# Weight sums of the first feed-forward in 2 KB tiles, norm squares on ScalarE, bounded leads for weights, and 54 instead of 53 small tiles

## The chip, the core and the metric

One core of a Trainium2 chip runs the whole program. The metric is the device time of one execution in microseconds (us). The engines are named as in the profile: PE is TensorE (PEld its weight loads), DVE is VectorE, ACT is ScalarE, POOL is GpSimd, SP is the queue from which the loads are issued.

## The reference

A decoder layer over 512 tokens of width 1024, in float32:

```
x = x + 0.5 * swiglu(rmsnorm(x, ffn1_norm), ffn1_wgu, ffn1_wdown)   # d_ff 2816
h = rmsnorm(x, mix_norm);  z = h @ w_in         # q, k, v, conv (2 x 1024), gates (2 x 1024)
a = sliding_window_attention(q, k, v, sinks) @ attn_proj
c = silu(layernorm(causal_conv31(glu(zc)))) @ conv_proj
x = x + (sigmoid(ga) * a + sigmoid(gb) * c) @ w_out
x = x + 0.5 * swiglu(rmsnorm(x, ffn2_norm), ffn2_wgu, ffn2_wdown)
x = x + sigmoid(rmsnorm(x, ple_gate_norm) @ ple_gate_w) * rmsnorm(p @ ple_proj, ple_norm)
```

where `swiglu(h, w_gu, w_down)` is `(silu(g) * u) @ w_down` with `g, u` the halves of `h @ w_gu`, and `rmsnorm` divides by the root of the mean square over the 1024 features.

## The kernel before

Features lie on the 128 partitions: x is eight tiles of 128 x 512 (features x tokens). Every float32 operand of a product is split into an upper and a lower half in a rounded format (ACT copies src to hi, DVE or POOL computes lo = src - hi), and `mm3` issues three matmuls for a product: hi x hi, lo x hi, hi x lo. A weight piece is a load of 128 x 1024 into a raw tile and two 4 KB tiles, whi and wlo, of class hi and lo.

**Pairs.** In a feed-forward the first blocks of 128 columns of g and u are done plainly (four in the first, two in the second), the others in pairs of blocks (`pair`, line 952) by a scheme with seven products in place of eight. A pair loads four raw pieces A[f, kh] (three in class raw, which has three slots, the fourth in class k, which has two), builds four sums of them (`add`, line 965; each in two halves of 128 x 512, tiles f_s, on DVE or POOL as the planner likes), and splits seven "forms" (`form`, line 971): 1 and 2 and 4 are raw pieces, 6, 5, 7 and 3 are the sums. They are multiplied two at a time in the order (1, 2), (6, 5), (7, 3), 4: `both` runs g and u, and each `times` is 12 matmuls of 256 columns. A form holds one hi and one lo slot, of three each, from its split to its last matmul. The moving operands are the h tiles and activations that `sums` (line 881) prepares once. After 8, 16 and 22 blocks `down` (line 1035) multiplies by w_down, in eight groups, one for each x tile.

**Norms.** `next_norm` (line 1070) gives the last `down` of a feed-forward, and the output product of the mixer, a function `after(o)`. It splits the new x[o] into h tiles and has `SumSq.add` (line 802) square x[o] on POOL and add it on POOL to a tile in SBUF. The sum over partitions follows as small matmuls (mean_rstd; names _n_cs in the trace) and is spread over the partitions, or as matmuls with a matrix of 1/1024 (wide_rstd, for the last norm). The very first norm does it otherwise: squares on ACT (n_sq), added by DVE into a PSUM bank (n_acc).

**The planner.** No order is written out. `record()` lists all operations; `deadlines` (line 366) works back a latest start for each from the PE order of the pass before; `simulate` (line 395) lets each engine take the ready operation with the earliest due time, and `plan` (line 640) makes five passes and keeps the one with the shortest simulated span. Then every operation is issued in that order (line 1495: all rows carry the line of this loop, L1498, so they are told apart by their tiles). `can` (line 435) decides whether an operation may take its output tiles: a slot of the class must be free (`SLOTS`, line 648: 53 of class a, 2 KB each; 8 PSUM banks); of class a, one, three or six must stay free beside it when its slack is over 2, 6 or 20 us; and hi and lo tiles aren't taken when the slack is over AHEAD = 22 us. Class a holds the h tiles and prepared activations (hi and lo, 16 tiles each in a feed-forward), rb, the f_s sums and the tiles of a pair's evictions (g, u, U: two each). DVE and POOL instructions on SBUF are planned as excluding each other.

Of the kernel before, what the change touches and what calls it, by code (L numbers as in the profile page):

```python
# [12 lines left out]
AF = mybir.ActivationFunctionType  # L13
ALU = mybir.AluOpType
# [29 lines left out]
"""  # L44
POOLCH = (0, 2, 4)
WARM = 9
AHEAD = 22
MARGIN = 0.0

CAPS = {"cz": 2, "ct": 4}  # L50
# [175 lines left out]
class Program:  # L226
# [69 lines left out]
    def costs(self, op, eng=None):  # L296

        ins = op.reads
        o = op.writes[0] if op.writes else None
        n = max([v.free() for v in ([o] if o else []) + ins])  # L300
        psum = any(v.vt.cls == "ps" for v in op.writes + ins)
        eng = eng or op.eng
        op.lock = eng == "POOL"
        op.fset = None
        op.dma = 0.0
        vecs = sum(isinstance(v, V) for v in [*op.a[3:], *(v for n, v in op.k.items() if n != "accum_out")])
        if eng == "PE":
            if op.what == "transpose":
                op.cost, op.lat = 0.112, 0.3
            else:  # L310
                n = op.a[2].free()
                if op.a[2].vt.dtype == F32R:
                    op.cost, op.lat = (0.2275, 0.3) if n > 256 else (0.121, 0.3)
                else:
                    op.cost, op.lat = max(0.15, n * 0.00167), 0.35
        elif eng == "DVE":
            op.lat = 0.15
            if op.what == "tensor_tensor":
                op.cost = 0.065 + n * 1.055e-3
            elif op.what == "scalar_tensor_tensor":  # L320
                op.cost = 0.08 + n * 1.12e-3
            elif op.what == "tensor_tensor_reduce":
                op.cost = 0.28 + n * 1.02e-3
            elif op.what in ("reduce_sum", "tensor_reduce"):
                op.cost = 0.08 + n * 1.03e-3
            else:
                op.cost = 0.08 + n * (1.25e-3 if psum else 0.9e-3)
            op.lock = not psum and op.what not in ("tensor_tensor_reduce", "reduce_sum", "tensor_reduce", "reciprocal")
        elif op.what == "dma_start" and eng == "ACT":
            op.cost, op.lat = 0.5, 2.6  # L330
        elif eng == "ACT":
            op.cost, op.lat = 0.07 + n * 0.88e-3, 0.17
            op.cost += 0.094 * vecs
            if "accum_out" in op.k:
                op.cost += 0.1
            f = op.a[2].name if len(op.a) > 2 else "Copy"
            op.fset = SETS.get(f)
        elif eng == "POOL":
            op.lat = 0.15
            if op.what == "tensor_tensor":  # L340
                op.cost = 0.14 + n * 2.1e-3
            elif op.what == "tensor_scalar":
                op.cost = 0.25 + n * 0.8e-3
            else:
                op.cost = 0.12 + n * 1.0e-3
        else:
            op.cost, op.lat = 0.47, 0.0
            v = (op.writes + op.reads)[0]
            op.dma = v.free() * v.shape[0] * 4 / 240e3
# [45 lines left out]
def simulate(prog, slots):  # L395
# [39 lines left out]
    def can(op, slack):  # L435
        for vt in op.outs:
            if vt.slot is None:
                break
        else:
            return True  # L440
        need = {}
        for v in op.writes:
            vt = v.vt
            if vt.slot is None:
                need.setdefault(vt.cls, {})[vt] = True
        for c, vts in need.items():
            spare = 0
            if c == "a":
                if slack > 400.0:
                    return False  # L450
                spare = 0 if slack < 2.0 else 1 if slack < 6 else 3 if slack < 20 else 6
            if c in ("hi", "lo") and slack > AHEAD:
                return False
            if len(free[c]) < len(vts) + spare:
                return False
            if any(vt.kind and inuse[vt.kind] >= CAPS[vt.kind] for vt in vts):
                return False
        return True
# [89 lines left out]
    while left:  # L548
# [23 lines left out]
        for e in ENGINES:  # L572
            if busy[e] > t + 1e-9:
                continue
            if e == "PE":
                pe(t)
                continue
            best = None
            if e == "SP":
                state = len(ready[e]), len(free["raw"]), len(free["a"])  # L580
                if state == idle_sp:
                    continue
                idle_sp = state
            for key, _, op in ready[e]:
                if best is not None and key >= best[0]:
                    break
                if op.outs and op.outs[0].after > t:
                    continue
                if e == "ACT" and op.fset and op.fset != aset:
                    key += 1.5  # L590
                elif e == "DVE":
                    if op.flex:
                        key += 5.0
                    if op.lock:
                        key += max(0.0, lock_pool - t)
                if best is not None and key >= best[0]:
                    continue
                if can(op, op.ls + lag - t):
                    best = (key, op)
            if best is None:  # L600
                continue
            op = best[1]
            slack = op.ls + lag - t
            if hold[e] > t and slack > 10.0 and op.cost > 0.3:
                continue
            if e == "POOL" and slack > 8.0:
                if hold[e] > t:
                    push(hold[e], "wake")
                    continue
                if lock_dve > t and any(o.lock and ls + lag - t < 4.0 for ls, _, o in ready["DVE"]):  # L610
                    push(lock_dve, "wake")
                    continue
            idle_sp = None if e == "SP" else idle_sp
            ready[e].remove((op.ls, op.i, op))
            if op.flex:
                ready["POOL" if e == "DVE" else "DVE"].remove((op.ls, op.i, op))
                op.eng = e
                prog.costs(op)
            launch(op, t)
# [25 lines left out]
    return prog, spans[-1]  # L645


SLOTS = {"a": 53, "o": 4, "raw": 3, "hi": 3, "lo": 3, "ps": 8, "k": 2, "x": 8, "c": 100000}


def record():
    nc = Program()

    def ps_tile(name):
        return nc.tile(name, [P, S], F32, "ps")

    def ftile(name):
        return nc.tile(name, [P, S], F32, "a")
# [48 lines left out]
    def mm3(ps, w, x, start, stop, first=1, skip=False):  # L707

        nc.tensor.matmul(ps, w[first], x[0], start=start, stop=False, skip_group_check=skip)
        nc.tensor.matmul(ps, w[1 - first], x[0], start=False, stop=False, skip_group_check=skip)  # L710
        nc.tensor.matmul(ps, w[0], x[1], start=False, stop=stop, skip_group_check=skip)

    def part(w, s):
        return w[0][:, s], w[1][:, s]
# [83 lines left out]
    class SumSq:  # L798
# [3 lines left out]
        def add(self, v, on_act=False, accs=1):  # L802
# [11 lines left out]
                eng.tensor_tensor(acc, acc, to, op=ALU.add)  # L814
            self.n += 1


    warm = ps_tile("warm")
    with nc.group("warm"):
# [83 lines left out]
                    forms[f].append((hi[:, j * HS : (j + 1) * HS], lo[:, j * HS : (j + 1) * HS]))  # L903
        return forms

    def ffn(tag, wgu, wdown, h, gain, ss, after, cuts, wide, plain):

# [42 lines left out]
        def pair(i, T, new):  # L952
# [16 lines left out]
                    nc.flex.tensor_tensor(sm[n][c], *ab, op=op)  # L969

            def form(n, src):
                hi = nc.tile(f"whi_{wgu}{i}_{n}", [P, PIECE], F32R, "hi")
                lo = nc.tile(f"wlo_{wgu}{i}_{n}", [P, PIECE], F32R, "lo")
                if isinstance(src, list):
                    for c in range(2):
                        s = slice(c * S, (c + 1) * S)
                        split_into(hi[:, s], lo[:, s], src[c])
                else:
                    split_into(hi, lo, src)
                return hi, lo  # L980
# [13 lines left out]
            def times(m, n, w, b, to, start):  # L994
                with nc.group(f"{tag}_p{n}{i}_{m}"):
                    for k in range(4):
                        c = k * 256 + m * P
                        mm3(to[m], part(w, slice(c, c + P)), b[k], start and k == 0, k == 3, skip=n in (3, 4, 6, 7))

            def both(n1, s1, r1, n2, s2, r2, first):  # L1000
                w1, w2 = form(n1, s1), form(n2, s2)
# [68 lines left out]
    def next_norm(tag, gain):  # L1070
        h, ss = [], SumSq(f"{tag}_ss")

        def after(o):
            h.append(split(f"{tag}_h{o}", x[o], gain[:, o : o + 1]))
            ss.add(x[o])

        return h, ss, after

    h2, ss2, after = next_norm("mix", g_mix)
    ffn("f1", "wgu1", "wd1", h, g_ffn1, ss, after, 4, False, 4)  # L1080


    def proj(tag, key, i, h, nk=KD):
# [365 lines left out]


    h4, ss4, after4 = next_norm("pg", g_gate)
    ffn("f2", "wgu2", "wd2", h3, g_ffn2, ss3, after4, 1, False, 2)


    rb4 = None
# [142 lines left out]
```

## Time and profile before

| what | us |
|---|---|
| median of 3 runs (lowest, highest) | 1183.63 (1183.03, 1185.38) |
| the profiled execution | 1182.44 |
| its span, from the first to the last instruction | 1180.7 |
| PE busy | 1166.4 (99%), 6740 matmuls |
| DVE busy | 984.3 (83%) |
| ACT busy | 630.2 (53%) |
| POOL busy | 492.2 (42%) |

Stages by the span's clock: first feed-forward to 362 us (its pairs from 54 us, with down projections at 94 to 137, 222 to 266 and from 330 us), the mixer to about 798 us, the second feed-forward to about 1133 us, then the last gate. In the rows below, a row of a timeline gives the start, the busy time, the engine, the operation and its tiles, the count, and in brackets the idle time of the engine before it with what ended it. Tiles of the pairs are named f_g8a, f_u8b and so on by the first block of the pair; wlo_wgu and whi_wgu are the halves of a form, f_s a sum, raw_wgu a loaded piece. A matmul's row is longer than its distance to the next one.

### The profile page before, as it was taken

What the parts mean: (1) busy time and instruction counts of PE and PEld (TensorE: products, weight loads), DVE (VectorE), ACT (ScalarE), POOL (GpSimd) and SP (SyncE); (2) the same over time, 40 slices, a digit from 0 to 9 for tenths busy, and PEclk for the clock granted to TensorE, in tenths of its full rate; (3) what the DMA queues carried; (4) which work ended last, traced back from release to release, by engine and by line L of the source; (5) the groups of instructions that cost most, each with busy time, mean ns of one, the idle gap of its engine ahead of it and who ended that gap; (6) DMA issues with size and microseconds to landing.
All of it is one profiled execution on the core that took longest, in us unless ns stands there. A gap on an engine that the chain in (4) does not pass through costs nothing.

```text
span 1180.7 us, 17926 instructions
## 1 busy us (share of the span) xinstructions
PE 1166.4 (99%) x6740; PEld 1029.3 (87%) x6740; DVE 984.3 (83%) x1479; ACT 630.2 (53%) x1117; POOL 492.2 (42%) x444
## 2 busy tenths in 40 slices
PE   9999999999999999999999999999999999999998
PEld 7898899989988888888888888889998999899886
DVE  7996799769986898998999786689966997589876
ACT  7553255415544669989865673445542555245432
POOL 2330442023334896897899600444302241122340
PEclk9999999999999999999999999999999999999999
DMA  7424224333133221222222233232243224222331
GB/s 239 131 72 125 89 91 125 90 100 114 41 106 105 90 90 54 89 72 72 72 90 89 89 91 107 90 125 80 86 151 105 81 90 128 87 92 75 103 107 72
DMA packets 37815, 115.30 MB, mean 98 GB/s; under 512 B 4704, under 2 KB 9440, under 8 KB 37728
## 3 DMA queue, kind: packets, MB, share of 16 engines
q1 hardware_dynamic: 37584, 114.12, 30.4%
q8 instruction: 53, 0.87, 0.3%
q14 instruction: 34, 0.28, 0.1%
q10 hardware_dynamic: 144, 0.03, 0.0%
HBM read 112.04 MB, written 2.10 MB: 97 GB/s over the span
## 4 chain that ended last, share of the span: by engine, by line
PE 87%; DVE 7%; ACT 3%; issue 2%; DMA 1%; SPq 0%; DVEq 0%; ACTq 0%
PE f_d L1498 20%; PE ga L1498 4%; PE ap L1498 4%; PE cp L1498 4%; PE wo L1498 4%; PE cb L1498 3%; PE pg L1498 3%; PE ca L1498 3%; PE gb L1498 2%; DVE wlo_wgu L1498 2%; PE f_g L1498 2%; PE f_u L1498 2%; PE q1b L1498 2%; DVE cz L1498 2%; PE sc L1498 2%
## 5 line engine op out<-in xcount | busy, mean ns | idle before, releaser
L1498 POOL TENSOR_TENSOR f_s<-raw_wgu,raw_wgu 128x512 f32<-128x512 f32 x42 | 73.9, 1770 | 337.6 <-DVE f_d L1498 164.0
L1498 DVE TENSOR_TENSOR wlo_wgu<-f_s,whi_wgu 128x512 fp32r<-128x512 f32 x152 | 136.3, 931 | 15.3 <-ACT whi_wgu L1498 15.1
L1498 ACT ACTIVATE whi_wgu<-raw_wgu 128x1024 fp32r<-128x1024 f32 (+1 forms) x93 | 76.2, 834 | 102.9 <-PE f_d L1498 35.0
L1498 ACT ACTIVATE whi_wgu<-f_s 128x512 fp32r<-128x512 f32 x152 | 88.7, 625 | 58.9 <-PE f_d L1498 13.3
L1498 POOL TENSOR_TENSOR y<-y,ct 128x507 f32<-128x507 f32 (+27 forms) x90 | 114.2, 1292 | 5.8 <-ACT ct L1498 4.2
L1498 DVE TENSOR_TENSOR wlo_wgu<-raw_wgu,whi_wgu 128x1024 fp32r<-128x1024 f32 (+1 forms) x93 | 108.4, 1174 | 7.7 <-ACT whi_wgu L1498 7.2
L1498 DVE SCALAR_TENSOR_TENSOR cz<-u,dww,cz 128x510 f32<-128x510 f32 (+25 forms) x145 | 105.0, 734 | 2.5
L1498 ACT ACTIVATE whi_wd<-raw_wd 128x1024 fp32r<-128x1024 f32 (+1 forms) x48 | 47.4, 987 | 104.4 <-PE f_d L1498 90.5
L1498 DVE TENSOR_TENSOR f_d<-f_d,f_n_rb 128x512 f32<-128x512 f32 x48 | 33.5, 698 | 70.8 <-PE f_d L1498 70.6
L1498 POOL TENSOR_TENSOR f_s<-raw_wgu,f_s 128x512 f32<-128x512 f32 x28 | 46.1, 1650 | 58.0 <-DVE f_us L1498 28.4
L1498 DVE TENSOR_TENSOR wlo_wd<-raw_wd,whi_wd 128x1024 fp32r<-128x1024 f32 (+1 forms) x48 | 54.7, 1140 | 7.3 <-ACT whi_wd L1498 7.3
L1498 ACT ACTIVATE ct<-u,dww 128x505 f32<-128x505 f32 (+28 forms) x90 | 58.3, 702 | 2.2 <-DVE u L1498 2.1
L1498 POOL TENSOR_TENSOR f_s<-f_s,raw_wgu 128x512 f32<-128x512 f32 x24 | 38.8, 1618 | 18.3 <-DVE f_s L1498 6.0
L1498 ACT ACTIVATE f_gs<-f_gs 128x512 f32<-128x512 f32 x44 | 27.5, 626 | 29.6 <-DVE f_gs L1498 29.6
L1498 POOL TENSOR_TENSOR f_ss_sq<-x 128x512 f32<-128x512 f32 x8 | 8.7, 1084 | 80.5 <-DVE x L1498 80.5
L1498 DVE TENSOR_TENSOR f_s<-raw_wgu,raw_wgu 128x512 f32<-128x512 f32 x34 | 35.7, 1054 | 0.7 <-DVE f_a10l L1498 0.4
L1498 DVE SCALAR_TENSOR_TENSOR x<-f_d,x 128x512 f32<-128x512 f32 x48 | 32.7, 688 | 1.1
L1498 ACT ACTIVATE s<-s,m,q_r 128x128 f32<-128x128 f32 x64 | 30.9, 487 | 0.1
L1498 ACT ACTIVATE whi_wzc<-raw_wzc 128x1024 fp32r<-128x1024 f32 x16 | 17.0, 1060 | 26.1 <-issue 9.0
L1498 POOL TENSOR_TENSOR mix_ss_sq<-x 128x512 f32<-128x512 f32 x8 | 10.9, 1363 | 39.8 <-DVE x L1498 39.8
L1498 POOL TENSOR_TENSOR pg_ss_sq<-x 128x512 f32<-128x512 f32 x8 | 12.6, 1572 | 35.8 <-DVE x L1498 35.8
L1498 ACT ACT_TABLE_LOAD x20 | 25.7, 1283 | 1.6 <-PEq L1587 1.2
(1289 smaller groups left out, 4552.3 us busy)
## 6 DMA issues: line engine op xcount, KB each, us to landing
raw_wgu<-in_wgu SPq DMA_DIRECT2D x80, 512.0 KB, 3.7
raw_wd<-in_wd SPq DMA_DIRECT2D x32, 512.0 KB, 4.0
raw_wzc<-in_wzc SPq DMA_DIRECT2D x16, 512.0 KB, 3.6
raw_wzg<-in_wzg SPq DMA_DIRECT2D x16, 512.0 KB, 3.6
raw_wd<-in_wd SPq DMA_DIRECT2D x16, 384.0 KB, 3.2
raw_wgu<-in_wgu SPq DMA_DIRECT2D x32, 128.0 KB, 3.1
raw_wq<-in_wq SPq DMA_DIRECT2D x8, 512.0 KB, 3.5
raw_wap<-in_wap SPq DMA_DIRECT2D x8, 512.0 KB, 3.5
```

Source lines behind the costliest of these rows:

```text
L1498: getattr(engines[op.eng], op.what)(*a, **k)
```

## The change

Five edits. In the first feed-forward (`own` is true there, false in the second) the forms that are sums no longer take a whi and a wlo tile of 4 KB: each half gets its own hi and lo tile of class a, 2 KB each, so four for a form; `times` picks the half. `next_norm` calls `in_psum` in place of `add`: squares on ACT, added by DVE, the running sum in a PSUM bank and the last one in an SBUF tile. The bound on slack is given by class: 16 us for hi and lo, 24 us for raw and k, which had none. Class a has 54 slots. The planner's cost of a matmul is 0.2272 and 0.1197 us in place of 0.2275 and 0.121, and its look at SP's queue is renewed with each new microsecond.

```diff
-AHEAD = 22
+LEAD = {"hi": 16, "lo": 16, "raw": 24.0, "k": 24.0}
-                    op.cost, op.lat = (0.2275, 0.3) if n > 256 else (0.121, 0.3)
+                    op.cost, op.lat = (0.2272, 0.3) if n > 256 else (0.1197, 0.3)
-            if c in ("hi", "lo") and slack > AHEAD:
+            if slack > LEAD.get(c, 1e9):
                 return False
-                state = len(ready[e]), len(free["raw"]), len(free["a"])
+                state = len(ready[e]), len(free["raw"]), len(free["a"]), int(t)
-SLOTS = {"a": 53, "o": 4, "raw": 3, "hi": 3, "lo": 3, "ps": 8, "k": 2, "x": 8, "c": 100000}
+SLOTS = {"a": 54, "o": 4, "raw": 3, "hi": 3, "lo": 3, "ps": 8, "k": 2, "x": 8, "c": 100000}
+        def in_psum(self, v, last):
+            n = self.n = self.n + 1
+            to = ftile(f"{self.name}_sq{n}")
+            nc.scalar.activation(to, v, AF.Square)
+            if n == 1:
+                self.run, self.one = ps_tile(f"{self.name}_acc"), to
+            else:
+                a = self.one if n == 2 else self.run
+                nc.vector.tensor_tensor(to if n == last else self.run, a, to, op=ALU.add)
+            if n == last:
+                self.accs.append(to)
             def form(n, src):
+                if isinstance(src, list) and own:
+                    hi, lo = ([rtile(f"{tag}_w{p}{n}_{i}_{c}") for c in range(2)] for p in "hl")
+                    for c in range(2):
+                        split_into(hi[c], lo[c], src[c])
+                    return hi, lo
-                        mm3(to[m], part(w, slice(c, c + P)), b[k], start and k == 0, k == 3, skip=n in (3, 4, 6, 7))
+                        if isinstance(w[0], list):
+                            wk = part([p[k // 2] for p in w], slice(c % S, c % S + P))
+                        else:
+                            wk = part(w, slice(c, c + P))
+                        mm3(to[m], wk, b[k], start and k == 0, k == 3, skip=n in (3, 4, 6, 7))
-            ss.add(x[o])
+            ss.in_psum(x[o], KD)
-    ffn("f1", "wgu1", "wd1", h, g_ffn1, ss, after, 4, False, 4)
+    ffn("f1", "wgu1", "wd1", h, g_ffn1, ss, after, 4, False, 4, True)
-    ffn("f2", "wgu2", "wd2", h3, g_ffn2, ss3, after4, 1, False, 2)
+    ffn("f2", "wgu2", "wd2", h3, g_ffn2, ss3, after4, 1, False, 2, False)
```

## Rows read from the trace of the kernel before

**Rows 1.** The page: busy time and share of the span by engine.

```profile
PE 1166.4 (99%) x6740; PEld 1029.3 (87%) x6740; DVE 984.3 (83%) x1479; ACT 630.2 (53%) x1117; POOL 492.2 (42%) x444
```

**Rows 2.** The chain that ended last: start, duration, what, count.

```profile
76.81 1.44 PE f_u6b L1498 x12
...
94.09 43.55 PE f_d L1498 x192
...
222.63 43.55 PE f_d L1498 x192
...
329.94 32.67 PE f_d L1498 x144
```

**Rows 3.** Windows by stage: length, then PE, PEld, DVE, ACT, POOL busy (instructions).

```profile
0.00:138.00 138.00, 135.40 (x753) 117.85 (x754) 110.00 (x185) 68.30 (x129) 34.42 (x34) 1.00 0.43 135
138.00:223.00 85.00, 81.92 (x672) 80.81 (x672) 77.71 (x110) 45.10 (x82) 27.71 (x17) 1.00 0.30 92
223.00:267.00 44.00, 44.00 (x200) 36.58 (x199) 27.29 (x32) 10.62 (x13) 6.81 (x4) 1.00 0.38 122
267.00:330.00 63.00, 61.09 (x499) 59.99 (x498) 58.49 (x82) 33.65 (x63) 19.65 (x12) 1.00 0.21 70
330.00:363.00 33.00, 33.00 (x149) 27.40 (x148) 27.69 (x33) 12.86 (x17) 18.30 (x14) 1.00 0.39 117
363.00:812.00 449.00, 448.06 (x2107) 373.37 (x2106) 384.47 (x620) 297.34 (x558) 292.31 (x307) 1.00 0.28 89
812.00:1090.00 278.00, 277.64 (x1967) 261.99 (x1966) 229.33 (x327) 131.16 (x222) 69.75 (x42) 1.00 0.30 97
1160.00:1180.70 20.70, 15.51 (x69) 12.51 (x67) 12.40 (x22) 2.98 (x6) 0.00 (x0) 0.99 0.28 103
```

**Rows 4.** PE's waits: for what, us in total, times, the longest.

```profile
PE f_g10a L1498 <- DVE wlo_wgu L1498: 1.8, 2, 1.1
...
PE f_g16a L1498 <- DVE wlo_wgu L1498: 0.6, 1, 0.6
```

**Rows 5.** Timeline of ACT at the end of pair 10.

```profile
177.75 1.06 ACT L1498 ACTIVATE whi_wgu<-raw_wgu 128x1024 fp32r<-128x1024 f32 x1 [1.82 <-PE f_u10a L1498]
180.68 0.63 ACT L1498 ACTIVATE whi_wgu<-f_s 128x512 fp32r<-128x512 f32 x1 [1.87 <-PE f_u10b L1498]
```

**Rows 6.** Timeline of DVE and of POOL at the start of pair 10.

```profile
159.50 0.68 DVE L1498 TENSOR_TENSOR wlo_wgu<-f_s,whi_wgu 128x512 fp32r<-128x512 f32 x1
...
164.58 3.46 DVE L1498 TENSOR_TENSOR wlo_wgu<-f_s,whi_wgu 128x512 fp32r<-128x512 f32 x2
...
162.27 3.53 POOL L1498 TENSOR_TENSOR f_s<-raw_wgu,raw_wgu 128x512 f32<-128x512 f32 x2 [10.75 <-DMA raw_wgu<-in_wgu]
```

**Rows 7.** Tile f_s, 55 to 335 us (two rows) and 800 to 1090: ns min/median/max.

```profile
L1498 DVE TENSOR_TENSOR wlo_wgu<-f_s,whi_wgu x72: 674/687/1794, 55.2 to 321.2; 128x512 fp32r<-128x512 f32 x72
...
L1498 DVE TENSOR_TENSOR f_s<-raw_wgu,raw_wgu x11: 677/1772/1790, 63.5 to 276.7; 128x512 f32<-128x512 f32 x11
...
L1498 DVE TENSOR_TENSOR f_s<-raw_wgu,raw_wgu x22: 675/680/1782, 801.2 to 1068.7; 128x512 f32<-128x512 f32 x22
```

**Rows 8.** The norms' tiles: squares on POOL and ACT, additions on DVE, column sums.

```profile
L1498 POOL TENSOR_TENSOR mix_ss_sq<-x 128x512 f32<-128x512 f32 x8 | 10.9, 1363 | 39.8 <-DVE x L1498 39.8
...
L1498 ACT ACTIVATE n_sq<-x x8: 614/616/623, 15.2 to 20.1; 128x512 f32<-128x512 f32 x8
...
L1498 DVE TENSOR_TENSOR n_acc<-n_acc,n_sq x5: 685/694/700, 17.6 to 21.7; 128x512 f32<-128x512 f32 x5
...
L1498 PE MATMUL mix_n_cs<-ones,mix_ss_sq x8: 168/250/250, 374.1 to 374.8; 128*128 128x1 f32 x8
```

**Rows 9.** Timeline of POOL: the mix norm's last addition.

```profile
367.61 2.18 POOL L1498 TENSOR_TENSOR mix_ss_sq<-mix_ss_sq,mix_ss_sq 128x512 f32<-128x512 f32 x1
```

**Rows 10.** ACT in a down projection; the page's issues (KB, us to landing).

```profile
126.80 1.06 ACT L1498 ACTIVATE whi_wgu<-raw_wgu 128x1024 fp32r<-128x1024 f32 x1 [4.38 <-PE f_d L1498]
...
raw_wgu<-in_wgu SPq DMA_DIRECT2D x80, 512.0 KB, 3.7
```

More of the change, by code (lines that the diff above doesn't have):

```diff
@@ L904, in sums, with ffn @@
         return forms
-    def ffn(tag, wgu, wdown, h, gain, ss, after, cuts, wide, plain):
+    def ffn(tag, wgu, wdown, h, gain, ss, after, cuts, wide, plain, own):
         rb = None
```

## The prediction

> **What bounds the kernel now.** I read the page's busy times first [rows 1]: TensorE (PE) is busy 1166.4 of 1180.7 us, VectorE (DVE) follows with 83%. A busy PE is not yet a PE at its pace, because a matmul's row is longer than its distance to the next one. The chain of waits gives the pace [rows 2]: 12 matmuls of 256 columns take 1.44 us, 0.120 us each; 192 of 512 columns take 43.55 us, 0.227 us each. The change leaves every matmul, so all that it can win is time in which PE was off that pace. The windows by stage say where that is [rows 3]. PE is idle 2.60 us in the first 138 us (the first loads) and 5.19 us after 1160 us (the last output's evictions); neither is touched. From 363 to 812 us it is idle 0.94 us, in the second feed-forward's pairs (812 to 1090) 0.36 us of 278. What stands out is the first feed-forward's pairs: 3.08 us in 138 to 223 and 1.91 in 267 to 330. The whole loss is larger, since a gap is seen only after the modelled end of a matmul. A down projection ends at 94.09 + 43.55 = 137.64 us and the next begins at 222.63 [rows 2]: 84.99 us for pairs 8 to 14, which are by the code 4 pairs x 7 forms x 2 groups x 12 = 672 matmuls, 80.64 us at 0.120. 4.35 us are lost. From 222.63 + 43.55 = 266.18 to 329.94 us are 63.76 us for three pairs, 504 x 0.120 = 60.48: 3.28 us lost. **7.6 us, 0.65% of the span, is what the change's first part can reach.** PE's waits agree: four names, f_g10a the longest and f_g16a the shortest of them, each for DVE's wlo_wgu, the lower half of a form [rows 4].
>
> Why is wlo_wgu late there? Two things meet. ScalarE makes a whi_wgu only when PE is through with an older form: it sat idle 1.82 us until f_u10a, 1.87 us until f_u10b [rows 5]. There are three hi and three lo tiles; two forms are multiplied at once, so one form at most is ready ahead, and the next is split while PE needs it. And that split is then slow: a half takes DVE 0.68 us while GpSimd (POOL) is quiet, but from 164.58 us two took 3.46, beside POOL's sums that began at 162.27 [rows 6]. In the second feed-forward the same three tiles cost next to nothing: a sum on DVE takes 680 ns in the median there, 1772 ns in the first [rows 7], and DVE is busy 229 of 278 us (82%) against 77.71 of 85 (91%) and 58.49 of 63 (93%) [rows 3]. So the bound in the two stretches is DVE, with work that can't be done early.
>
> The Trainium skill says of POOL and DVE (SBUF — State Buffer, section "SBUF: two separate sides") that they share a pair of ports under an exclusive lock, held for a whole instruction, and that a DVE instruction with two SBUF inputs is among those that wait. The stretched splits agree with it [rows 6]. By it the norm's new additions, with one operand in PSUM, would keep their duration beside a busy POOL; by the stretch of the splits, 1.73 for 0.68, seven of them would cost DVE some 7 us more in a norm.
>
> **The change, part by part.**
> *Sums through 2 KB tiles.* The 8 splits of sums a pair stay, 72 in nine pairs on each of ScalarE and DVE [rows 7], and so do the loads. What goes is the wait for a hi tile in four of seven forms; three slots then serve forms 1, 2 and 4 alone in the 20.2 us of a pair (14 groups of 1.44). A split can start when its sum is there. DVE has room beforehand: in the down projection ahead it is busy 27.29 of 44 us [rows 3]. The bounds are 0 (as late as now) and 7.6 us (as in the second feed-forward). A new limit speaks against all of it. By the code 16 h tiles, 16 of prepared activations and rb are held throughout, so 54 - 33 = 21 are free; a pair takes 6 for evictions, 8 for sums and now 16 for split sums, 30 if all lived at once. The two forms in work hold 8, the evictions 6; 7 are left for what is ahead: a form and a half, not a pair. I take two thirds, nearer to the second feed-forward's row, because the late splits miss by little (1.1 us at the longest [rows 4]): **-5.1 us**.
>
> *Squares and their sum.* Each of three norms loses 8 squares and 7 additions on POOL, in the mix norm 8 x 1.363 = 10.9 us and 7 x some 1.6 (the last took 2.18 [rows 9]). It gains 8 squares on ScalarE at 616 ns and 7 additions into PSUM on DVE at 694 ns, 4.9 us each [rows 8]. In 330 to 363 us ScalarE is busy 12.86 of 33 us and DVE 27.69 [rows 3], so 32.6 with the additions if nothing came back; but POOL's 18.30 us there all but vanish, and each of its operations could hold up a split by a microsecond [rows 6]: some 3 to 5 us. On the path it is nothing: POOL's last addition ends at 369.8 us and PE comes to mix_n_cs only at 374.1, behind the key and value products [rows 8, 9]. If that cover went, a square and an addition would show, 1.3 us. A new wait comes in: each addition waits on DVE for ScalarE's square, which may stand behind a whi of 1.06 us [rows 10], and behind the addition stand the next x and h_l, which PE needs after the last group. I take 0; bounds -0.5 and +2.
>
> *Leads.* In a down projection the slots bind before the leads do: ScalarE waits 4.38 us for PE f_d to let a hi tile go, two pieces of 5.4 us (43.55 / 8) ahead of its use, inside 16; a load lands in 3.7 us [rows 10], far inside 24. SP issues in order, so a load held back holds those behind it. I take 0; bounds -0.5 and +1, for stretches of attention in which a split held back meets a full DVE or leaves it to something more urgent. *One more tile* adds no instruction; its worth is in the 21 above.
>
> *A new order.* The planner's costs of a matmul and its look at SP change too, so the order of the middle moves. Between 363 and 1090 us there are 0.94 + 0.36 = 1.3 us to win [rows 3]; what a bad order costs is shown by the pairs 8 to 14, 4.35 us. I take 0, bounds -1.3 and +4.3.
>
> Sum: the profiled execution took 1182.44 us (the span of 1180.7 and 1.74 around it); 1182.44 - 5.1 = 1177.3. The median of the runs, 1183.63, is 1.2 us above this execution, so **1178.5 us** as a median.
>
> **Rivals.** (a) The tiles are merely swapped: 7 left are short of the 8 of the next pair's sums, which start later than now, and the splits stay as late. For it: POOL already sat 10.75 us until raw_wgu came [rows 6], so raw tiles are let go late. Against it: hi and lo come free for the raw forms, which empty raw tiles sooner. With a loss of 4 to 9 us in place of 7.6 that is 1180 to 1185, at 7.6 us 1183.6.
> (b) Slower: the 2 KB tiles run dry. Sums wait until a form has been multiplied; then two dependent additions on POOL (2 x 1.77), a whi (0.63) and a wlo (0.68) follow, 4.8 us against 2.88 for the form in work [rows 2, 5, 6]. 1.9 us in each of nine pairs is 17 us in place of 7.6: 1193. It decides from the point at which the next pair's sums find no free tile until PE is through with a form. The Trainium skill's page Perfetto Trace Analysis (section "Identifying Performance Opportunities") says that one gap repeating on the engine that should be full can mean that buffers ran out. So far the gaps differ from pair to pair, 1.8 us before f_g10a and 0.6 before f_g16a [rows 4].
> (c) Slower in the middle: the gain is there, but the new order costs 4.3 us, the fuller DVE of the norms 2 and the leads 1 us: 1178.5 + 7.3 = 1185.8 and up.
>
> **How the numbers follow.** About 0.2%, 2.4 us, is what a measurement here can tell from no change. The forecast (1176 to 1181.2) has 0.58, a still larger gain (under 1176: all 7.6 and some of the middle) 0.05, (a) 0.21, (b) 0.07, (c) 0.09. Of (a) 0.02 lies under 1181.3, of (c) 0.02 under 1186.0. So faster is 0.58 + 0.05 + 0.02 = 0.65, same 0.19 + 0.02 = 0.21, slower 0.07 + 0.07 = 0.14. The range goes from the full gain with 1.3 us of the middle, 1183.6 - 8.9 = 1174.7, to the lower end of (c), 1186.0; outside are (b), most of (c) and a little below.
>
> **What would show it.** Right: PE's waits no longer name f_g10a to f_g18a for a wlo, pairs 8 to 14 take 81 to 83 us and pairs 16 to 20 60.5 to 62, ScalarE no longer waits for PE before the whi of a sum, POOL has no squares. The first step is wrong if the stretches are still 85 and 64 us; then POOL waits longer for raw_wgu (a), or gaps come in every pair (b). The second is wrong if PE waits at mix_n_cs or at the first group of the last gate, the others if PE idles over 2 us in 363 to 812 us.

## The result, and the profile after

The changed kernel takes 1174.33 us in the median of four runs (1172.64 to 1176.13), the kernel before 1184.27 beside it: ratio 0.9917, 95% interval 0.9898 to 0.9935. That is the direction of the forecast, and 0.4 us below its range. The profiled execution took 1174.18 us, its span 1172.4.

First the chain of waits of the changed kernel (start, duration, what, count). A down projection ends at 93.16 + 43.55 = 136.71 us and the next begins at 217.48; the one after ends at 261.03 and is followed at 321.50.

```profile
93.16 43.55 PE f_d L1522 x192
...
217.48 43.55 PE f_d L1522 x192
...
321.50 32.67 PE f_d L1522 x144
```

So pairs 8 to 14 take 80.77 us in place of 84.99 and pairs 16 to 20 take 60.47 in place of 63.76 [rows 2]. The pace is 80.64 and 60.48: **nothing is left of the 7.6 us.** From here on I call the two "stretch 1" and "stretch 2" and read them off PE's timeline, from the first matmul of the first pair to the first of the next down projection. The windows between these points, in the columns of [rows 3], show PE without any idle time:

```profile
136.54:217.32 80.78, 80.78 (x674) 80.68 (x672) 76.15 (x108) 43.54 (x77) 36.87 (x23) 1.00 0.32 103
260.87:321.34 60.47, 60.47 (x506) 60.47 (x504) 55.04 (x82) 32.54 (x58) 24.67 (x16) 1.00 0.30 91
```

DVE, the third engine in the row, is busy 76.15 of 80.78 us, 94%; before it was 91% [rows 3]. The engine that I called the bound is fuller than before, and PE no longer waits for it in the pairs. PE's longest waits (for what, us in total, times, the longest) are all elsewhere, against [rows 4]:

```profile
PE sc L1522 <- DVE qT_l L1522: 2.0, 1, 2.0
PE warm L1522 <- DVE ones L1522: 1.1, 1, 1.1
PE f_u L1522 <- ACT f_n_rb L1522: 0.7, 1, 0.7
PE f_g2a L1522 <- ACT f_gs L1522: 0.6, 1, 0.6
```

In stretch 1 (136 to 217 us) ScalarE hardly waits any more for PE to let a tile go before it copies a sum (0.7 and 0.2 us): f_wh, the new hi tile, waits for the sum itself. A whi, now for raw forms alone, waits for PE 1.8 us in two times at the most; in [rows 5] each of two such waits took that long.

```profile
ACT f_gs L1522 <- DVE f_gs L1522: 10.6, 5, 3.7
ACT f_wh L1522 <- POOL f_s L1522: 3.7, 5, 1.1
ACT f_wh L1522 <- DVE f_s L1522: 3.1, 2, 2.5
ACT whi_wgu L1522 <- PE f_u12b L1522: 1.8, 2, 1.0
```

The collisions of DVE with POOL are still there. On the timelines of the two in pair 10, two splits take 3.49 us beside POOL's sums, as long as in [rows 6]. Of the 72 splits of sums, 31 take over 0.75 us after the change and 25 before it; each of them has work on POOL beside it.

```profile
166.63 3.49 DVE L1522 TENSOR_TENSOR f_wl<-f_s,f_wh 128x512 fp32r<-128x512 f32 x2
...
166.24 5.03 POOL L1522 TENSOR_TENSOR f_s<-raw_wgu,raw_wgu 128x512 f32<-128x512 f32 x3 [10.09 <-DVE f_us L1522]
```

The norms went as the diff says (against [rows 8]): squares on ScalarE, sums on DVE, and PE comes to mix_n_cs at 365.5 us, long after the last of them at 358.3 + 0.68.

```profile
L1522 ACT ACTIVATE mix_ss_sq<-x x8: 615/616/619, 327.7 to 356.9; 128x512 f32<-128x512 f32 x8
L1522 PE MATMUL mix_n_cs<-ones,mix_ss_sq x8: 168/250/250, 365.5 to 366.2; 128*128 128x1 f32 x8
L1522 DVE TENSOR_TENSOR mix_ss_acc<-mix_ss_acc,mix_ss_sq x5: 685/691/693, 336.7 to 354.2; 128x512 f32<-128x512 f32 x5
L1522 DVE TENSOR_TENSOR mix_ss_sq<-mix_ss_acc,mix_ss_sq x1: 676/676/676, 358.3 to 358.3; 128x512 f32<-128x512 f32 x1
```

PE's timeline accounts for the 8.3 us between the two spans: the start up to the first down projection -0.94 (93.93 to 92.99 us; 0.77 of it lies ahead of the first pair), stretch 1 -4.21, stretch 2 -3.29, the mixer from the end of the third down projection to its output product +0.66 (379.15 to 379.81), the second feed-forward -0.03, the last gate's products -0.47 (44.27 to 43.80), the end -0.02.

### The profile page after: what moved, and what is told of

It is laid out like the page before. It is cut to its first block, busy times and chain, and to the rows that moved or that the text cites. A ratio compares the mean times of both kernels' runs of the same rounds, so it can differ in the third digit from the quotient of the medians.

```text
span 1172.4 us, 17962 instructions
## 1 busy us (share of the span) xinstructions
PE 1161.6 (99%) x6740; PEld 1029.6 (88%) x6740; DVE 973.4 (83%) x1481; ACT 639.7 (55%) x1139; POOL 456.2 (39%) x418
## 4 chain that ended last, share of the span: by engine, by line
PE 94%; ACT 2%; DVE 2%; POOL 1%; issue 1%; DMA 0%; SPq 0%; DVEq 0%; ACTq 0%
PE f_d L1522 20%; PE ap L1522 4%; PE ga L1522 4%; PE pg L1522 4%; PE cp L1522 4%; PE wo L1522 4%; PE ca L1522 3%; PE gb L1522 3%; PE cb L1522 3%; PE f_u L1522 2%; PE f_g L1522 2%; PE q1b L1522 2%; PE q0b L1522 2%; PE sc L1522 2%; PE f_u14b L1522 1%; PE f_u20b L1522 1%
## 5 line engine op out<-in xcount | busy, mean ns | idle before, releaser
L1522 POOL TENSOR_TENSOR f_s<-raw_wgu,raw_wgu 128x512 f32<-128x512 f32 x51 | 86.6, 1710 | 345.5 <-DMA raw_wgu<-in_wgu 115.6
L1522 DVE SCALAR_TENSOR_TENSOR cz<-u,dww,cz 128x504 f32<-128x504 f32 (+25 forms) x145 | 104.7, 732 | 2.3
L1522 DVE TENSOR_TENSOR f_wl<-f_s,f_wh 128x512 fp32r<-128x512 f32 x72 | 71.4, 1012 | 1.5 <-ACT f_wh L1522 1.0
L1522 POOL TENSOR_TENSOR f_s<-raw_wgu,f_s 128x512 f32<-128x512 f32 x31 | 52.3, 1694 | 51.6 <-DVE f_us L1522 20.6
L1522 DVE TENSOR_TENSOR wlo_wgu<-f_s,whi_wgu 128x512 fp32r<-128x512 f32 x80 | 66.3, 863 | 6.0 <-ACT whi_wgu L1522 5.8
L1522 ACT ACTIVATE whi_wgu<-f_s 128x512 fp32r<-128x512 f32 x80 | 46.6, 625 | 32.4 <-PE f_d L1522 8.9
L1522 ACT ACTIVATE f_wh<-f_s 128x512 fp32r<-128x512 f32 x72 | 43.6, 626 | 26.6 <-DVE f_s L1522 12.9
L1522 POOL TENSOR_TENSOR f_s<-f_s,raw_wgu 128x512 f32<-128x512 f32 x31 | 49.2, 1594 | 20.8 <-DVE f_s L1522 6.0
L1522 POOL TENSOR_TENSOR f_t<-x 128x256 f32<-128x256 f32 x8 | 6.5, 807 | 86.8 <-DVE x L1522 81.6
L1522 ACT ACTIVATE whi_wzg<-raw_wzg 128x1024 fp32r<-128x1024 f32 x16 | 17.1, 1069 | 16.9 <-PE ga L1522 5.0
```

Of the source, the lines that this page charges most:

```text
L1522: getattr(engines[op.eng], op.what)(*a, **k)
```

## The experiments

All times are medians, all ratios are to the kernel before on the same chip. The stretches come from each run's own profile; the pace is 80.64 and 60.48 us.

| run | first feed-forward's sums | 2 KB tiles for split sums | stretch 1, 2 | us | ratio (95%) |
|---|---|---|---|---|---|
| before | DVE and POOL | no | 84.99, 63.76 | 1183.96 to 1185.21, by chip | 1 |
| changed | DVE and POOL | yes | 80.78, 60.47 | 1174.33 | 0.9917 (0.9898, 0.9935) |
| e1 | DVE and POOL | no, all else changed | 84.12, 62.17 | 1179.43 | 0.9958 (0.9945, 0.9971) |
| e2 | DVE and POOL | yes, nothing else changed | 80.78, 61.19 | 1177.16 | 0.9938 (0.9926, 0.9951) |
| e3 | DVE and POOL | no, planner's costs alone | 83.93, 64.02 | 1183.42 | 1.0003 (0.9993, 1.0014) |
| e4 | DVE and POOL | no, norms alone | 86.76, 64.46 | 1184.64 | 1.0000 (0.9989, 1.0011) |
| e5 | DVE and POOL | two of four sums | 80.64, 60.47 | 1175.45 | 0.9927 (0.9906, 0.9948) |
| e6 | DVE and POOL | at most nine tiles | 80.63, 62.76 | 1176.47 | 0.9937 (0.9915, 0.9959) |
| e7 | DVE | no, nothing else changed | 80.63, 60.47 | 1175.83 | 0.9930 (0.9913, 0.9947) |
| e8 | DVE and POOL | yes, other leads | 80.79, 60.65 | 1173.65 | 0.9910 (0.9894, 0.9926) |
| e9 | POOL | no, nothing else changed | 87.27, 67.65 | 1189.93 | 1.0041 (1.0027, 1.0054) |
| e10 | POOL | yes | 80.63, 60.47 | 1172.89 | 0.9900 (0.9883, 0.9917) |
| e11 | DVE | yes, other leads | 80.63, 60.47 | 1173.15 | 0.9900 (0.9886, 0.9913) |
| e12 | DVE | no, other leads | 80.64, 60.48 | 1174.90 | 0.9912 (0.9898, 0.9925) |

**Which part carries it (e1 to e4).** Theory T was that the small tiles take the stalls away, by letting a split start early; the rival O was that the other edits happen to give a better order. In the cuts of diffs here and below, a line with # says which kernel is edited.

```diff
 # e1: the changed kernel
-    ffn("f1", "wgu1", "wd1", h, g_ffn1, ss, after, 4, False, 4, True)
+    ffn("f1", "wgu1", "wd1", h, g_ffn1, ss, after, 4, False, 4, False)
 # e2: the kernel before, with own, form and times of the change; SLOTS, AHEAD, norms, costs as before
 # e3: the kernel before
-                    op.cost, op.lat = (0.2275, 0.3) if n > 256 else (0.121, 0.3)
+                    op.cost, op.lat = (0.2272, 0.3) if n > 256 else (0.1197, 0.3)
 # e4: the kernel before, with in_psum
-            ss.add(x[o])
+            ss.in_psum(x[o], KD)
```

> The changed kernel with one part taken back: the first feed-forward's sums go through whi and wlo again; norms, leads, 54 tiles and the planner's costs stay as changed. Stretch 1 is the PE time of pairs 8 to 14 (84.99 us before, 80.77 after, 80.64 at pace), stretch 2 that of pairs 16 to 20 (63.76, 60.47, 60.48). Theory T (the small tiles take the stalls away): stretches back at about 85 and 64, f_g10a or the like waits for wlo_wgu, time about 1182. Rival O (the other edits give an order in which DVE and POOL collide less, the tiles are not needed): stretches under 82 and 61.5, time 1174 to 1176.

> The kernel before with one part put in: the first feed-forward's sums go through 2 KB tiles (53 of them); norms on POOL, lead 22 for hi and lo, old planner costs. T: stretches at 81 and 60.5 as after the change, time about 1176.5. O: the tiles alone do not bring the stretches to their pace, at least one stays 2 us or more above it, time over 1180.

> The kernel before with only the planner's two costs of a matmul changed (0.2275 to 0.2272, 0.121 to 0.1197): the same instructions, in another order. T: stretches stay near 85 and 64, give or take 1, time 1182 to 1185. O: the order alone can take 2 us or more off the stretches; time down to 1177 to 1181.

> The kernel before with only the norms' squares on ScalarE and their sum in PSUM. T: stretches near 85 and 64 (the norms come after them), time within 2 us of before. O: since the plan is made anew, the stretches may move by 2 us or more in either direction although no norm lies in them; time 1178 to 1186.

In e2 the tiles alone bring stretch 1 from 84.99 to 80.78 us and stretch 2 from 63.76 to 61.19, 6.8 of the 7.5 us. Without them (e1) the rest of the change leaves 84.12 and 62.17: 2.5 us less than before. So e1 lies between the two expectations, in stretch 1 nearer to T's 85, in stretch 2 nearer to O's 61.5, and in the time (1179.43) between 1176 and 1182; it is e2 that speaks against O (1177.16 us, and O had over 1180). The tiles' share thus depends on the order of counting: 6.8 us when they are put in first, 5.0 (146.29 to 141.25 us for both stretches) when they are put in last. The windows of e1 and then of e2 show it on PE, first column after the length:

```profile
137.00:221.12 84.12, 81.90 (x673) 80.91 (x672) 78.25 (x111) 45.75 (x83) 26.77 (x17) 1.00 0.26 82
264.67:326.84 62.17, 61.45 (x505) 60.72 (x504) 58.73 (x83) 34.48 (x63) 20.54 (x12) 1.00 0.24 80
```

```profile
137.83:218.61 80.78, 80.78 (x673) 80.68 (x672) 74.49 (x109) 43.51 (x77) 31.87 (x22) 1.00 0.34 115
262.16:323.35 61.19, 60.73 (x505) 60.52 (x504) 55.81 (x85) 32.31 (x58) 20.40 (x14) 1.00 0.31 99
```

O is true in the small: a new order alone moved stretch 1 by -1.1 (e3) and +1.8 us (e4), without an edit in it. Neither changed the time beyond its interval. The norms are worth something in one place: the last gate's products take 43.80 or 43.81 us from the first to the last matmul in the nine kernels that sum in PSUM (the changed one, e1, e4, e5, e6, e8, e10, e11 and e12) and 44.26 to 44.31 in the five that don't (before, e2, e3, e7, e9). There pg_h_l is no longer held up by POOL's squares: one takes DVE 742 ns in the median after the change and 1518 before, and PE's wait for it, 0.2 us, is gone from the list.

**How much of the tiles is needed (e5, e6).** In e5 only forms 6 and 5 use them; in e6 at most nine may be in use at once.

```diff
 # e5
-                if isinstance(src, list) and own:
+                if isinstance(src, list) and own and n in (6, 5):
 # e6
-CAPS = {"cz": 2, "ct": 4}
+CAPS = {"cz": 2, "ct": 4, "xw": 9}
-                    hi, lo = ([rtile(f"{tag}_w{p}{n}_{i}_{c}") for c in range(2)] for p in "hl")
+                    hi, lo = ([rtile(f"xw_{tag}_{p}{n}_{i}_{c}") for c in range(2)] for p in "hl")
```

> The changed kernel, but only two of the four sum forms (6 and 5) use the 2 KB tiles; 7 and 3 go through whi and wlo again, which then serve five forms of a pair instead of three (seven without the small tiles). Stretch 1 (pairs 8 to 14) was 80.78 us with all four, 84.12 with none (the run without small tiles), stretch 2 60.47 and 62.17. T (what helps is that a form can be split before PE is through with an older one): half of the relief is enough or nearly so: 80.7 to 82 and 60.4 to 61.2. If each form in the small tiles is worth its own share of the stall instead, the stretches lie half way, 82.5 and 61.3.

> The changed kernel with at most nine of the 2 KB tiles in use by split sums at one time: two forms and one tile, so practically none can be split while two are multiplied. Nothing else changes. T: the lead is gone and the stalls come back, larger than before the change, as the rival (b) of the prediction describes it: stretch 1 at 84 us or more, stretch 2 at 62.5 or more, PE waits for f_wl before the second forms of pair after pair. If the gain came from something else of the small tiles (smaller pieces, reads from other addresses), the stretches stay at 81 and 60.5.

e5 came out as T has it: half the relief removes the whole stall. e6 went against what T expected. With nine tiles stretch 1 stays at pace (80.63) and only stretch 2 loses 2.3 us (62.76, no better than the 62.17 of e1 without any); I had expected stalls in pair after pair. But e6 took away less of the lead than was meant. I take the splits in the order in which the forms are multiplied, and measure from the end of a form's second half to PE's first matmul with the form. For forms 5 and 3, the second of each two, the lead is in the median 4.6 and 1.6 us in the changed kernel and still 1.7 and 1.4 in e6; in the kernel before, form 5 is ready 0.2 us ahead and form 3 is 0.3 us late. So e6 doesn't show that something other than an early start matters; that is for e7.

**The other half (e7).** The rival P was that the collisions of DVE with POOL cause the stalls.

```diff
 # e7: the kernel before
-                    nc.flex.tensor_tensor(sm[n][c], *ab, op=op)
+                    (nc.vector if tag == "f1" else nc.flex).tensor_tensor(sm[n][c], *ab, op=op)
```

> The kernel before with the first feed-forward's sums on DVE alone, so that POOL does nothing in its pairs and no split on DVE is stretched by it. Rival P (the collisions of DVE with POOL cause the stalls): stretch 1 under 82.5, stretch 2 under 62, time 4 us or more under before. T (the late start behind the hi and lo tiles causes them, the collisions only add to it): DVE takes over 17 sums of 0.61 us and loses the stretches, its load stays; stretches 83 to 86 and 62.5 to 65.

T's expectation failed, and P's held. With three hi and three lo tiles, as before, and the sums all on DVE, both stretches are at their pace and the time is 0.9930 of before. DVE has 125 instructions in stretch 1 where it had 110, and is busy 71.48 us where it was 77.53:

```profile
137.19:217.82 80.63, 80.63 (x673) 80.63 (x672) 71.48 (x125) 45.40 (x81) 0.00 (x0) 1.00 0.31 92
...
L1498 DVE TENSOR_TENSOR wlo_wgu<-f_s,whi_wgu x72: 679/685/694, 54.4 to 313.2; 128x512 fp32r<-128x512 f32 x72
```

The second row is tile f_s in e7: not one of 72 splits takes longer than 694 ns, where [rows 7] has up to 1794. The same window of the kernel before, for the comparison:

```profile
137.48:222.47 84.99, 81.91 (x674) 80.89 (x673) 77.53 (x110) 45.09 (x81) 27.71 (x17) 1.00 0.30 93
```

The late start is still there in e7. In stretch 1 ScalarE waits 21.0 us for PE before a whi, where it waited 22.2 before, and forms 5 and 3 are ready only 0.4 and 0.7 us ahead in the median. In pair 10, PE comes to form 5 (f_g10a) 1.09 us after DVE began its two splits and doesn't wait, because they take 1.29 us together and the second half is used half a group later. In the kernel before they took 3.46 [rows 6]; PE was through with the group before 0.75 us after their start, and waited 1.07 us for the first and 0.71 for the second. The first three rows are of e7, the last is of the kernel before:

```profile
ACT whi_wgu L1498 <- PE f_u10b L1498: 5.2, 3, 3.0
...
163.45 1.29 DVE L1498 TENSOR_TENSOR wlo_wgu<-f_s,whi_wgu 128x512 fp32r<-128x512 f32 x2
...
164.54 0.28 PE L1498 MATMUL f_g10a<-f_t_h,wlo_wgu 128*128 128x256 f32 x1
```

```profile
166.40 0.39 PE L1498 MATMUL f_g10a<-f_t_h,wlo_wgu 128*128 128x256 f32 x1 [1.07 <-DVE wlo_wgu L1498]
```

**Both together (e9 to e12).** The theory N that follows from this: a stall needs a split that starts late, behind the hi and lo tiles, and a POOL sum that holds it up. Either remedy is enough. It was tested by more collisions without (e9) and with (e10) the small tiles, and by none with (e11) and without (e12) them.

```diff
 # e9: the kernel before; e10: the changed kernel
-                    nc.flex.tensor_tensor(sm[n][c], *ab, op=op)
+                    (nc.gpsimd if tag == "f1" else nc.flex).tensor_tensor(sm[n][c], *ab, op=op)
 # e11, e12: the changed kernel; e12 with own = False besides
+                    (nc.vector if tag == "f1" else nc.flex).tensor_tensor(sm[n][c], *ab, op=op)
+LEAD = {"hi": 18, "lo": 18, "raw": 24.0, "k": 30.0}
```

> The kernel before with the first feed-forward's sums on POOL alone, whi and wlo for all forms. Theory N, formed after the earlier runs: a stall needs both, a split that starts late behind the hi and lo tiles and a POOL sum that holds it up; take either away and PE keeps its pace (small tiles alone did, sums on DVE alone did). N here: more collisions and the same late start, stretch 1 (84.99 us before) at 86 or more, stretch 2 (63.76) at 64.5 or more, time 2 us or more over before. Rival D (DVE's own load is what is short in the pairs): DVE loses its share of the sums, so the stretches get shorter, under 84 and 63.

> The changed kernel, small tiles and all, with the first feed-forward's sums on POOL alone. N: the early start covers the collisions also when there are more of them: stretches under 82 and 61.5, time within 2 us of the changed kernel (1174.3). If the early start covers only what the changed kernel happens to have, the stretches come to 83 and 62 or more and the time to over 1177.

> The changed kernel with the first feed-forward's sums on DVE alone and the leads 18, 18, 24, 30. N: stretches at their pace, 80.7 and 60.5; POOL idle in the pairs; 1171 to 1174.5, the best so far or level with it (1173.65 with other leads alone).

> As the run with small tiles and sums on DVE alone, but without the small tiles: whi and wlo for all forms. N: without collisions the small tiles are not needed, stretches within 0.5 us of that run, 80.7 and 60.5, time within 1 us of it. If the early start is worth something by itself, it is 2 us or more slower.

N held in all four for the stretches, and rival D (that DVE's own load is what is short) fell. First e9, then e10:

```profile
138.08:225.35 87.27, 82.47 (x673) 81.03 (x672) 80.46 (x101) 45.04 (x81) 43.52 (x26) 1.00 0.30 98
268.90:336.55 67.65, 63.30 (x506) 62.27 (x504) 61.05 (x78) 34.77 (x63) 29.65 (x18) 0.97 0.23 76
```

```profile
136.68:217.31 80.63, 80.63 (x674) 80.63 (x672) 77.11 (x101) 43.53 (x78) 45.41 (x27) 1.00 0.30 99
260.86:321.33 60.47, 60.47 (x506) 60.47 (x504) 57.30 (x79) 33.19 (x60) 31.66 (x19) 1.00 0.29 94
```

The same 101 instructions on DVE in stretch 1, the same sums on POOL: with late splits PE loses 6.6 us, with early ones nothing, at a DVE that is busy 96% (77.11 of 80.63). The two differ in all the edits of the change, but each has its own pair with the sums where the planner put them: the kernel before (84.99) and the changed one (80.78). Stretch 2 of e9 is a less clean measure: PE was idle for 3.0 of the 8 us from 304 to 312 us, and from about 310.1 to 313.5 us the granted clock was 0.50, the lower of its two levels (1.2 GHz). There 17 matmuls took 3.52 us in place of 2.04, so 1.5 of the 7.2 us over the pace are the clock's. In e10 even the median split is stretched, 1054 ns:

```profile
L1522 DVE TENSOR_TENSOR f_wl<-f_s,f_wh x70: 675/1054/1837, 49.0 to 310.7; 128x512 fp32r<-128x512 f32 x70
```

e12 keeps the pace without the tiles; its time is 1.75 us above that of e11, outside the 1 us expected, though not in the stretches. Between the two profiles, 2.1 us apart, 1.1 us lies in the mixer (378.87 and 377.80 us) and 1.3 after the start of the last matmul (6.9 and 5.6 us), where the stores of the output took 2.4 and 1.7 us to land in the median of two.

**A better version (e8, e10, e11).** e8 changes the planner's bounds alone:

```diff
-LEAD = {"hi": 16, "lo": 16, "raw": 24.0, "k": 24.0}
+LEAD = {"hi": 18, "lo": 18, "raw": 24.0, "k": 30.0}
-WINDOW = 10
+WINDOW = 12
```

> The changed kernel with other bounds for the planner: 18 us for hi and lo, 24 for raw, 30 for k, and 12 instead of 10 groups among which PE's next one is chosen. A trial at a better version, no test of T: stretches stay at their pace (81, 60.5); the middle, where the changed kernel lost 2.4 us before one sc group, gets another order. 1171 to 1176.

e8, e10 and e11 reach 0.9910, 0.9900 and 0.9900. The changed kernel loses 2.0 us before one sc group, where DVE has a stretched split and five steps of the convolution in front of qT_l:

```profile
498.60 3.50 DVE L1522 TENSOR_TENSOR wlo_wzg<-raw_wzg,whi_wzg 128x1024 fp32r<-128x1024 f32 x1
502.02 3.28 DVE L1522 SCALAR_TENSOR_TENSOR cz<-u,dww,cz 128x501 f32<-128x501 f32 x5
```

That wait is in none of the three. In e10 the last matmul starts at 1164.80 us, in the changed kernel at 1166.84, but in e8 it starts at 1166.83: what e8 gains in the mixer it has lost elsewhere in its profile. The intervals overlap that of the changed kernel, so by the times none of them is shown to be faster than it.

## Why the prediction was right in its mechanism and short in its size

- **Where the loss was, and its size, right.** 7.6 us were worked out from the chain and the count of matmuls; 7.5 us of them were won.
- **The step that failed: "I take two thirds", -5.1 us, the sum's only term for the two stretches.** Measured: 148.75 to 141.25 us for both stretches, -7.5; -6.8 with the tiles alone (e2). Two thirds were taken out of fear that 7 free tiles would not do. The 54 slots were enough, and in the changed kernel two forms in small tiles (e5) do all of it. Only at nine tiles (e6) does the fear come true, and then in stretch 2 alone. A cause that misses "by little" is gone with a little more lead; a share of the loss was the wrong kind of estimate. That the late splits miss by 1.1 us at the longest was an argument for the whole.
- **"So the bound in the two stretches is DVE" was wrong.** DVE at 96% (e10) holds nobody up. That is rival D of e9, which fell. "Two things meet" was right, and stronger than it was meant: e7 and e2 take one of the two away each; e7 removes the whole loss, e2 all but 0.7 us of it.
- **Rivals.** (a) did not happen. (b), the tiles running dry, did not either; the run nearest to it, with nine tiles (e6), lost 2.3 us in one stretch, far from the 17 us of its price. (c) has a true core: the mixer lost 0.66 us, with a single wait of 2.0 us.
- **Norms: 0 taken, -0.47 us in the last gate**, at the edge of the bounds. The covers named (key and value products) held. What was not seen is that pg_h_l itself was held up by POOL's squares. That an addition with one operand in PSUM keeps its duration beside a busy POOL was hardly tested: POOL did nothing during these additions in the changed kernel (685 to 693 ns), and the one in e4 with 0.62 us of POOL beside it took 684 ns.
- **A new order: 0 taken.** The start gained 0.94 us, which the text had as not touched because of "the first loads", and the mixer gave 0.66 back. That reading was wrong: before the first pair PE's list names no load, but DVE's ones (1.1 us), wlo_wgu (0.6), h_l (0.5) and n_sq (0.3), and in the changed kernel ScalarE's f_n_rb (0.7) and wlo_wgu (0.2) stand in the place of the last three. "Four names" in the list is also short: f_g18b, with 0.4 us for wlo_wgu, is a fifth in the stretches, and f_g4a, with 0.4, waits likewise in the first pair.
- **From the profiled execution to the median: 1.2 us were added, 0.15 were there** (1174.18 and 1174.33). The executions of one kernel differ by more than a microsecond, and the offset of one kernel's profile is nobody else's.

The sum: -2.4 (7.5 instead of 5.1), -0.8 (start, mixer, gate), -1.0 (the offset) are -4.2 us, the distance from 1178.5 to 1174.3. With the first alone in its place the forecast would have been 1176.1, inside its range; the start, the gate and the offset carry the result 0.4 us out of it, which is less than the four runs differ by.

## What to carry to other kernels

Where an engine is held up by an operand that is made just in time, ask for each of its two causes what it takes to remove it: an earlier start (more places to put the result) or a faster making (no collision). Removing either one took the stall away here (e7 in full, e2 but for 0.7 us), so a share of the loss is a poor estimate: the loss goes to nothing as soon as the lead exceeds the delay. And an engine's busy share does not make it the bound: splits at 91% of DVE stalled PE, at 96% with a lead they did not.

## What the runs showed of the hardware that I had not expected

A second engine can cost the first more than it takes over. From e11 to e10, which differ in the planner's leads besides, DVE hands its sums in stretch 1 to POOL (127 to 101 instructions, 25 of them sums), and DVE's busy time rises. The window of e11:

```profile
136.85:217.48 80.63, 80.63 (x674) 80.63 (x672) 71.79 (x127) 43.25 (x77) 0.00 (x0) 1.00 0.32 105
```

71.79 against 77.11 us in e10. With 0.685 us for a sum on DVE (its median in e7) 25 sums are 17.1 us that left DVE, and 5.3 us came on top: (17.1 + 5.3) / 25 = 0.9 us of DVE's busy time for each sum on POOL, more than doing it costs. It is an estimate from above, since rows on DVE overlap a little. e7 and e9 point the same way and differ in nothing else: 71.48 us with the sums on DVE, 80.46 with them on POOL, though over a longer stretch.

The Trainium skill (SBUF — State Buffer, section "SBUF: two separate sides") says why they collide: the port pair that the two share is locked for a whole instruction. The traces agree, with 0.68 us for a split alone and up to 1.8 beside POOL. What they add is the price worked out above.
